# Two layers of a diffusion backbone on one core: modulation sums ordered behind the row scaling, the gate row multiplied ahead of the row factor, attention masks grouped, four weight differences on GpSimd

## The chip, the cores and the metric

The kernel runs on one core of a Trainium2 chip. The metric is the device time of one execution in microseconds (us); the time before is the median of three runs. The profile is one execution, taken by the hardware profiler.

## The reference, cut to what matters

512 tokens of width 1024 (256 context, 256 latent) go through two layers. Each layer is half-step SwiGLU, token mixer, half-step SwiGLU; every part is normed before and after, scaled and shifted by modulation vectors, and gated by one:

```python
def modulate(h, g_pre, shift, scale):
    return rms_norm(h, g_pre) * (1 + scale) + shift

def modulation(cond, w, b):                      # w: 1024 x 9*1024 per layer
    m = jax.nn.silu(cond) @ w + b

def half_ffn_update(h, mod, k, g_pre, g_post, w_in, w_out):
    y = swiglu(modulate(h, g_pre, mod[3 * k], mod[3 * k + 1]), w_in, w_out)
    return h + FFN_RES_WEIGHT * mod[3 * k + 2] * rms_norm(y, g_post)
...
x = x + mx[5] * rms_norm(yx, g[4])               # after the mixer
```

The mixer of layer 0 is a gated linear recurrence in both directions (RG-LRU), that of layer 1 is windowed attention (16 heads of 64, 4 key heads, a sink per head). The context has its own modulation. D_FF is 2816. All is float32. Only the latent half is returned.

## The kernel before, in words

**Precision.** Every large matmul is done as three: a value is split into a rounded high part (ScalarE copies it to fp32r, `split`, L113) and the rest (VectorE subtracts the high part). A weight slot (`wslot`, L117) is one load of 128 x 1024 floats into one of five `raw` buffers, a cast `whi` on ScalarE (L114) and a difference `wlo` on VectorE (L115), in one of eight slots. Activations are held as `hh` and `hl`.

**Tiling.** The tokens are four tiles of 128 rows: tiles 2 and 3 are latent (LAT), 0 and 1 context (CTX), worked in the order 2, 3, 0, 1. An FFN (L446) first does four blocks of 128 columns of the gate and up products for LAT, then the same four for CTX (a unit is 24 matmuls of 128x256), then the other 18 blocks for all tokens, in three groups; after each group the rows are multiplied by that part of `w_out` and added into `y`.

**Boundary.** In the last group, `out_last` (L427) finishes tile after tile; `after(t)` then calls `post` (L204: square and sum on ScalarE, an inverse root by small steps on VectorE (`rstd`, L175), product with the gate row and the row factor, add into the residual `x`) and `pre` (L218: square, inverse root, and the row scaling `scaled`, L192, whose last instruction is L194). The eight transposes of the scaled tile (`turn`, L197, matmul L201) follow as `pre_turn` some units later; ScalarE then applies scale and shift (L239) and the split makes `hh` and `hl`, which the next stage multiplies. So the next stage's LAT units start while the CTX tiles are still being normed.

**Modulation.** The next parts' modulation vectors are computed beside the FFN, as jobs (`mod_job`, L354) from which a step function takes one piece after each block or unit. A job clears two accumulators (one for each condition, memset L359; they lie in the two `m4` buffers), puts the bias into row 0 by a DMA from GpSimd's queue, and then for each of 8 rows of weight blocks loads 128 x 1024 floats and adds them times a per-partition scalar (L365, one for each condition). The column sums are matmuls with ones (L371). A gate row (`f` given) is multiplied by the norm's weights and written to DRAM, from where it is later read as a row for all partitions; a shift or scale is copied by ScalarE (L392) and transposed to columns (L280, then L396).

**Order.** The kernel is written against a framework that lays out each engine's queue when the kernel is built: a planner simulates the engines and takes the instruction that is ready and of highest priority; `pre` and `post` run at high priority. Semaphores are set by it. Each engine then runs its queue in order. Weight and modulation loads are all issued by SyncE, in its queue's order.

**Attention.** `soft` (L866) makes the scores of four heads and 128 queries in eight steps: for each of two pairs of heads two products of 64 rows (L877), two matmuls that add the mask through the identity (L879), then row maximum, exponential, and sum. Transposes and value products of the step before last stand between.

**Last FFN.** `last_ffn` (L957) starts with the token tiles as stationary operand and eight weight slots; at its end `finish` (L977) norms each tile, adds the residual and stores it.

The lines around which the change turns:

```python
for c in conds:
    v.scalar_tensor_tensor(acc[c], raw, self.cs[:, k, c : c + 1], acc[c], op0=ALU.mult, op1=ALU.add)
...
nc.vector.scalar_tensor_tensor(tmp, ysrc, r, grow[cond], op0=ALU.mult, op1=ALU.mult)
nc.vector.tensor_tensor(self.x[:, t], self.x[:, t], tmp, op=ALU.add)
```

Of the kernel before, what the change touches and what calls it, by code (L numbers as in the profile page):

```python
# [36 lines left out]
class Net:  # L37
    def __init__(self, ctx, tc):
# [4 lines left out]
        self.pending = []  # L43
        e = ctx.enter_context
# [68 lines left out]
    def split(self, hi, lo, src):  # L113
        self.nc.scalar.copy(hi, src)  # L114
        self.nc.vector.tensor_tensor(lo, src, hi.bitcast(F32), op=ALU.subtract)  # L115

    def wslot(self, srcs):  # L117
# [9 lines left out]
        self.split(hi[:, :n], lo[:, :n], raw[:, :n])  # L127
# [64 lines left out]
    def scaled(self, t, xs):  # L192
        r = self.rstd([self.mean_sq(xs, self.x[:, t])])
        self.nc.vector.tensor_scalar(xs, self.x[:, t], r, RS, op0=ALU.mult, op1=ALU.mult)  # L194
        return xs
# [157 lines left out]
    def mod_job(self, l, m, conds=(0, 1), f=None):  # L353
# [7 lines left out]
        for k in range(NK):  # L361
            raw = self.raw()
            nc.sync.dma_start(raw, self.w_mod[l, k * P : (k + 1) * P, m * D : (m + 1) * D])
            for c in conds:
                v.scalar_tensor_tensor(acc[c], raw, self.cs[:, k, c : c + 1], acc[c], op0=ALU.mult, op1=ALU.add)  # L365
            yield
        ps = self.st()
# [10 lines left out]
        if f is not None:  # L378
            gq = self.s2()
            gi = 3 + m // 3  # L380
            for j in range(4):
                cc = slice((j // 2) * 512, (j // 2) * 512 + 512)
                nc.gpsimd.dma_start(gq[32 * j : 32 * j + 32], self.norm_g[l, gi : gi + 1, cc].to_broadcast((32, 512)))
            row = self.a2()
# [713 lines left out]
```

## Time and profile before

| what | value |
|---|---|
| median of 3 runs | 1713.89 us (1711.07 to 1714.55) |
| the profiled execution | 1710.77 us, of which 1709.0 us span |
| TensorE busy | 1658.0 us (97%) |
| VectorE busy | 1118.7 us (65%) |
| ScalarE busy | 704.7 us (41%) |
| GpSimd busy | 44.2 us (3%) |
| loads | 253 MB, 148 GB/s on average |

The span is the time from the first to the last event that the profiler saw on the core. PE is TensorE (PEld its weight loads), DVE VectorE, ACT ScalarE, POOL GpSimd, SP SyncE; a q behind a name (SPq) means its sequencer. A line such as L115 is one of the kernel's source lines; a helper such as `split` has one line for all its callers, and the tile names tell them apart. `PEclk` is the clock granted to TensorE as a share of 2.4 GHz.

### The profile page before, as it was taken

The page shows a single profiled execution, that of the slowest core. Times are in us where ns is not written, and L with a number is a line of the kernel's source. Part 1 is how long each engine was busy: PE and PEld are TensorE (multiplying, and loading weights), DVE is VectorE, ACT ScalarE, POOL GpSimd, SP SyncE. Part 2 cuts the span into 40 slices and gives each one's busy share as a digit, 9 for nine tenths or more (in the row PEclk, how much of TensorE's full clock was granted, in tenths as well). Part 3 has the DMA queues.
Part 4 walks back from the last instruction along what each step waited for, and adds up shares of the span by engine and source line. Part 5 has one row for each costly group of instructions (what it writes and reads, how often), then busy time and mean ns, then how long its engine had stood idle before and what let it go on. Part 6 is the DMA issues. An engine that isn't in the chain of part 4 may idle for free.

```text
span 1709.0 us, 22391 instructions
## 1 busy us (share of the span) xinstructions
PE 1658.0 (97%) x8744; PEld 1385.9 (81%) x8744; DVE 1118.7 (65%) x1705; ACT 704.7 (41%) x1117; POOL 44.2 (3%) x89
## 2 busy tenths in 40 slices
PE   6999999999999989999999999999999999999997
PEld 4978888888988788888888888878888886679997
DVE  4878677658978785877833695655433687575454
ACT  3423322236699442332222442332232466574442
POOL 0010000000000001000000001000000000000000
PEclk9999999999999999999999999999999999999999
DMA  9366655443233154666433055865332061046561
GB/s 341 132 207 214 202 174 177 147 162 99 79 95 99 50 198 133 211 205 198 156 116 98 26 197 164 293 197 172 108 109 96 29 218 50 1 152 210 169 202 45
DMA packets 163961, 253.39 MB, mean 148 GB/s; under 512 B 9600, under 2 KB 114664, under 8 KB 163856
## 3 DMA queue, kind: packets, MB, share of 16 engines
q1 hardware_dynamic: 159424, 244.35, 43.8%
q0 software_dynamic: 3680, 7.10, 1.4%
q8 instruction: 68, 1.11, 0.3%
q10 hardware_dynamic: 752, 0.53, 0.1%
q14 instruction: 37, 0.30, 0.1%
HBM read 250.84 MB, written 1.10 MB: 147 GB/s over the span
## 4 chain that ended last, share of the span: by engine, by line
PE 77%; DVE 10%; ACT 5%; DMA 5%; issue 2%; ACTq 0%; DVEq 0%
PE mm L151 15%; PE mm L153 15%; PE mm L152 15%; PE mm L166 7%; PE mm L168 7%; PE mm L167 7%; DVE m L365 3%; DMA raw<-in_w_mod_dram 2%; DVE wlo L115 2%; PE mm L877 1%; DMA raw<-in_ffn_w_out_dram 1%; DMA raw<-in_ffn_w_in_dram 1%; ACT whi L114 1%; PE st L914 1%; PE st L903 1%
## 5 line engine op out<-in xcount | busy, mean ns | idle before, releaser
L151 PE MATMUL mm<-hh,whi 128*128 128x512 f32 (+1 forms) x1808 | 615.8, 342 | 8.3 <-ACT hh L271 4.7
L152 PE MATMUL mm<-hl,whi 128*128 128x512 f32 (+1 forms) x1808 | 615.7, 341 | 1.4 <-DVE hl L115 1.0
L153 PE MATMUL mm<-hh,wlo 128*128 128x512 f32 (+1 forms) x1808 | 616.3, 341 | 0.3 <-DVE wlo L115 0.3
L115 DVE TENSOR_TENSOR wlo<-raw,whi 128x1024 fp32r<-128x1024 f32 x316 | 382.4, 1221 | 157.0 <-ACT whi L114 155.3
L114 ACT CAST whi<-raw 128x1024 fp32r<-128x1024 f32 x316 | 330.2, 1053 | 353.4 <-DMA raw<-in_ffn_w_in_dram 107.5
L151 PEld LDWEIGHTS mm<-hh,whi 128*128 128x128 f32 x1808 | 346.0, 192 | 54.4 <-ACT hh L271 5.4
L152 PEld LDWEIGHTS mm<-hl,whi 128*128 128x128 f32 x1808 | 346.5, 192 | 39.5 <-DVE hl L115 1.4
L153 PEld LDWEIGHTS mm<-hh,wlo 128*128 128x128 f32 x1808 | 346.8, 192 | 38.1 <-DVE wlo L115 0.6
L365 DVE SCALAR_TENSOR_TENSOR m<-raw,cs,m 128x1024 f32<-128x1024 f32 x224 | 277.0, 1278 | 47.1 <-DMA raw<-in_w_mod_dram 39.2
L166 PE MATMUL mm<-whi,dh 128*128 128x512 f32 x592 | 232.7, 393 | 4.7 <-ACT dh L114 2.4
L168 PE MATMUL mm<-whi,dl 128*128 128x512 f32 x592 | 231.2, 391 | 0.0
L167 PE MATMUL mm<-wlo,dh 128*128 128x512 f32 x592 | 231.0, 390 | 0.0
L413 DVE TENSOR_TENSOR a<-s,mm 128x512 f32<-128x512 f32 (+1 forms) x96 | 54.5, 568 | 171.0 <-PE mm L153 111.8
L166 PEld LDWEIGHTS mm<-whi,dh 128*128 128x128 f32 x592 | 111.6, 188 | 34.0 <-issue 3.4
L412 ACT ACTIVATE s<-mm 128x512 f32<-128x512 f32 (+1 forms) x96 | 48.3, 503 | 214.1 <-PE mm L153 214.1
L168 PEld LDWEIGHTS mm<-whi,dl 128*128 128x128 f32 x592 | 111.6, 188 | 23.9 <-DVE dl L115 0.4
L167 PEld LDWEIGHTS mm<-wlo,dh 128*128 128x128 f32 x592 | 111.5, 188 | 22.4
L114 ACT CAST dh<-a 128x512 fp32r<-128x512 f32 (+1 forms) x96 | 50.5, 526 | 187.6 <-DVE a L413 187.6
L115 DVE TENSOR_TENSOR dl<-a,dh 128x512 fp32r<-128x512 f32 (+1 forms) x96 | 54.6, 569 | 26.5 <-ACT dh L114 26.3
L239 ACT ACTIVATE tmp<-st,modT,A 128x128 f32<-128x128 f32 x144 | 54.6, 468 | 9.3 <-PE st L201 9.3
L482 DVE TENSOR_TENSOR y<-y,mm 128x512 f32<-128x512 f32 x24 | 16.5, 686 | 38.1 <-PE mm L168 38.1
L172 ACT ACTIVATE tmp<-y 128x1024 f32<-128x1024 f32 x12 | 12.7, 1058 | 58.5 <-DVE y L434 58.5
(212 smaller groups left out, 1311.6 us busy)
## 6 DMA issues: line engine op xcount, KB each, us to landing
raw<-in_ffn_w_in_dram SPq DMA_DIRECT2D x176, 512.0 KB, 4.8
raw<-in_w_mod_dram SPq DMA_DIRECT2D x128, 512.0 KB, 4.4
raw<-in_ffn_w_out_dram SPq DMA_DIRECT2D x88, 512.0 KB, 4.8
wm<-in_w_mod_dram SPq DMA_DIRECT2D x16, 512.0 KB, 7.2
raw<-in_rg_w_in_dram SPq DMA_DIRECT2D x16, 512.0 KB, 3.3
raw<-in_attn_w_qkv_dram SPq DMA_DIRECT2D x12, 512.0 KB, 3.7
g<-spill POOLq DMA_DIRECT2D x16, 256.0 KB, 4.4
raw<-in_rg_gate_w_dram SPq DMA_DIRECT2D x16, 256.0 KB, 3.2
```

Of the source, the lines that this page charges most:

```text
L114: self.nc.scalar.copy(hi, src)
L115: self.nc.vector.tensor_tensor(lo, src, hi.bitcast(F32), op=ALU.subtract)
L151: nc.tensor.matmul(out, a, xh, start=first and k == ks[0], stop=False, skip_group_check=True)
L152: nc.tensor.matmul(out, a, xl, start=False, stop=False, skip_group_check=True)
L153: nc.tensor.matmul(out, b, xh, start=False, stop=last and k == ks[-1], skip_group_check=True)
L166: nc.tensor.matmul(out, a, wh, start=(k == 0), stop=False)
L167: nc.tensor.matmul(out, a, wl, start=False, stop=False)
L168: nc.tensor.matmul(out, b, wh, start=False, stop=(k == nk - 1))
L239: nc.scalar.activation(hf[:, k * P : (k + 1) * P], ps[:, q * P : (q + 1) * P], AF.Identity, bias=S[:, k, cond : cond + 1], scale=A[:, k, c ...
L365: v.scalar_tensor_tensor(acc[c], raw, self.cs[:, k, c : c + 1], acc[c], op0=ALU.mult, op1=ALU.add)
L412: nc.scalar.activation(a, pg, AF.Silu)
L413: nc.vector.tensor_tensor(b, a, pu, op=ALU.mult)
```

## The change

1. `mod_job`: the sums (L365) are traced in a block that tells the planner to queue them on VectorE behind `self.chain`, the row scaling of the tile that was normed last. In the first FFN there is none yet.
2. The column sum of a job (`mod_sum`) and the transposes to columns (`mod_cols`) are no longer pieces of the job. They are put into a list and done at the start of the next step each; a job so has 8 pieces instead of 9 or 10. Behind the last group the list is emptied.
3. `post` and `finish`: VectorE multiplies `y` by the gate row without waiting for the row factor; then one instruction multiplies by the factor and adds the residual. The squares' output goes to an `m4` buffer. `finish` stores the second half from ScalarE's queue.
4. A one-column Silu behind the last Gelu of the RG mixer and behind the last exponential of the attention.
5. `soft`: all four products of a step first, then all four masks.
6. Last FFN: of the first eight weight slots, the second and the fourth of each four have their difference on GpSimd.

```diff
     def post(self, t, ysrc, grow):
-        nc = self.nc
-        tmp = self.tmp()
-        cond = t // 2
+        v = self.nc.vector
+        g = grow[t // 2]
+        tmp, junk = self.tmp(), self.m4().rearrange("p a b -> p (a b)")
+        parts = []
         if isinstance(ysrc, list):
-            halves = [slice(cb * 512, cb * 512 + 512) for cb in range(2)]
-            r = self.rstd([self.mean_sq(tmp[:, cc], y) for cc, y in zip(halves, ysrc)])
-            for cc, y in zip(halves, ysrc):
-                nc.vector.scalar_tensor_tensor(tmp[:, cc], y, r, grow[cond][:, cc], op0=ALU.mult, op1=ALU.mult)
+            for cb, y in enumerate(ysrc):
+                cc = slice(cb * 512, cb * 512 + 512)
+                parts.append(self.mean_sq(junk[:, cc], y))
+                v.tensor_tensor(tmp[:, cc], y, g[:, cc], op=ALU.mult)
         else:
-            r = self.rstd([self.mean_sq(tmp, ysrc)])
-            nc.vector.scalar_tensor_tensor(tmp, ysrc, r, grow[cond], op0=ALU.mult, op1=ALU.mult)
-        nc.vector.tensor_tensor(self.x[:, t], self.x[:, t], tmp, op=ALU.add)
+            parts.append(self.mean_sq(junk, ysrc))
+            v.tensor_tensor(tmp, ysrc, g, op=ALU.mult)
+        r = self.rstd(parts)
+        v.scalar_tensor_tensor(self.x[:, t], tmp, r, self.x[:, t], op0=ALU.mult, op1=ALU.add)

     def pre(self, t, A, S, buf):
         with self.tc.high_priority():
             xs = self.scaled(t, buf)
+        self.chain = self.last
...
             for c in conds:
-                v.scalar_tensor_tensor(acc[c], raw, self.cs[:, k, c : c + 1], acc[c], op0=ALU.mult, op1=ALU.add)
+                with self.order(self.chain):
+                    v.scalar_tensor_tensor(acc[c], raw, self.cs[:, k, c : c + 1], acc[c], op0=ALU.mult, op1=ALU.add)
+            if k == NK - 1:
+                self.later.append(lambda: self.mod_sum(l, m, acc, f))
             yield
+
+    def mod_sum(self, l, m, acc, f):
...
+        if f is None:
+            row = self.s2()
+            nc.scalar.copy(row, ps)
+            self.later.append(lambda: self.mod_cols(l, m, row))
             return
...
+    def finish_later(self):
+        todo, self.later = self.later, []
+        for f in todo:
+            f()
...
         def step(n):
+            N.finish_later()
             while n > 0:
...
+    with N.order(prev):
+        sc.activation(N.small([P, 1]), c1[:, 0:1], AF.Silu)
...
-        for c in range(2):
-            ps = [N.mm() for _ in range(2)]
+        banks = [[N.mm() for _ in range(2)] for _ in range(2)]
+        for c, ps in enumerate(banks):
             for i in range(2):
                 half = slice(64 * i, 64 * i + 64)
                 nc.tensor.matmul(ps[i], qf[2 * g + c][half, qs], kk[g][half], start=True, stop=False)
+        for ps in banks:
             for i in range(2):
                 nc.tensor.matmul(ps[i][:, mc], identr, mask[:, qt], start=False, stop=True)
+        for c, ps in enumerate(banks):
...
+        if u == 7:
+            sc.activation(N.small([P, 1]), es[:, 0:1], AF.Silu)
...
-        for cb in range(2):
-            ss.append(N.mean_sq(tmp[:, cb * 512 : cb * 512 + 512], po[t, cb]))
-        r = N.rstd(ss)
+        tmp, junk = N.tmp(), N.m4().rearrange("p a b -> p (a b)")
         for cb in range(2):
             cc = slice(cb * 512, cb * 512 + 512)
-            v.scalar_tensor_tensor(tmp[:, cc], po[t, cb], r, grow[1][:, cc], op0=ALU.mult, op1=ALU.mult)
-            v.tensor_tensor(tmp[:, cc], tmp[:, cc], N.x[:, 2 + t, cc], op=ALU.add)
-            nc.sync.dma_start(out[0, t * P : (t + 1) * P, cc], tmp[:, cc])
+            ss.append(N.mean_sq(junk[:, cc], po[t, cb]))
+            v.tensor_tensor(tmp[:, cc], po[t, cb], grow[1][:, cc], op=ALU.mult)
+        r = N.rstd(ss)
+        for cb, q in ((0, nc.sync), (1, nc.scalar)):
+            cc = slice(cb * 512, cb * 512 + 512)
+            v.scalar_tensor_tensor(tmp[:, cc], tmp[:, cc], r, N.x[:, 2 + t, cc], op0=ALU.mult, op1=ALU.add)
+            q.dma_start(out[0, t * P : (t + 1) * P, cc], tmp[:, cc])
...
-    first = [N.wrows(vi, 0, NK, 0), N.wrows(vi, 0, NK, 0, DFF)]
+    first = [
+        [N.wslot([vi[:, k : k + 2, c0 : c0 + 512]], nc.gpsimd if k in (2, 6) else None) for k in range(0, NK, 2)]
+        for c0 in (0, DFF)
+    ]
```

## Rows read from the trace of the kernel before

**Rows 1.** The page's busy time of each engine (share of the span) xinstructions.
```profile
PE 1658.0 (97%) x8744; PEld 1385.9 (81%) x8744; DVE 1118.7 (65%) x1705; ACT 704.7 (41%) x1117; POOL 44.2 (3%) x89
```
**Rows 2.** Waits of TensorE: instruction <- releaser: us in total, times, longest.
```profile
PE st L201 <- DVE y L194: 5.7, 4, 2.5
...
PE st L280 <- ACT s L392: 2.6, 1, 2.6
...
PE st L201 <- DVE tmp L194: 1.9, 1, 1.9
PE st L201 <- DVE small L183: 1.6, 1, 1.6
PE mm L166 <- ACT hh L114: 1.6, 1, 1.6
```
**Rows 3.** Stretches: length, busy us (instructions) by engine, PEclk, DMA share, GB/s.
```profile
608.20:634.62 26.42, 20.10 (x165) 19.26 (x163) 26.42 (x47) 13.11 (x31) 0.00 (x0) 0.98 0.51 171
634.62:640.50 5.88, 5.88 (x28) 5.88 (x29) 3.03 (x3) 0.00 (x0) 0.00 (x0) 0.51 0.55 177
640.50:646.38 5.88, 5.88 (x52) 5.88 (x51) 1.90 (x3) 2.46 (x4) 0.00 (x0) 1.00 0.00 1
1009.40:1019.18 9.78, 5.64 (x25) 4.83 (x25) 9.78 (x14) 4.83 (x12) 0.00 (x0) 0.65 0.51 161
1143.19:1148.96 5.77, 3.18 (x10) 2.56 (x10) 4.44 (x7) 1.10 (x2) 0.00 (x0) 0.70 0.88 296
1148.96:1152.00 3.04, 3.04 (x15) 2.50 (x14) 0.00 (x0) 0.00 (x0) 0.49 (x1) 1.00 0.52 199
```
**Rows 4.** VectorE's sums by line in 608:637.7 (busy us, mean ns | idle before).
```profile
L365 DVE SCALAR_TENSOR_TENSOR m<-raw,cs,m 128x1024 f32<-128x1024 f32 x16 | 20.3, 1278 | 0.0
```
**Rows 5.** VectorE in order of time: start, us, instruction; RG mixer to FFN.
```profile
608.02 1.28 DVE L365 SCALAR_TENSOR_TENSOR m<-raw,cs,m 128x1024 f32<-128x1024 f32 x1
...
627.77 1.28 DVE L365 SCALAR_TENSOR_TENSOR m<-raw,cs,m 128x1024 f32<-128x1024 f32 x1
628.97 0.74 DVE L194 TENSOR_SCALAR y<-xres,small 128x1024 f32<-128x1024 f32 x1
```
**Rows 6.** SyncE's queue in order of time, the loads of block 4.
```profile
624.75 9.61 SPq L123 DMA_DIRECT2D raw<-in_ffn_w_in_dram  x4
```
**Rows 7.** TensorE in order of time, transposes in the two boundaries without sums.
```profile
433.02 1.09 PE L201 MATMUL st<-ident,y 128*128 128x128 f32 x8 [1.36 <-DVE y L194]
...
1374.50 1.09 PE L201 MATMUL st<-ident,y 128*128 128x128 f32 x8 [0.16 <-DVE y L194]
```
**Rows 8.** Line 359 alone: ns min/median/max, first and last start.
```profile
L359 DVE MEMSET m<- x28: 912/912/912, 65.2 to 1147.5; 128x1024 f32 x28
```
**Rows 9.** VectorE in order of time: a scan, then before the last FFN.
```profile
553.94 1.22 DVE L745 TENSOR_TENSOR_SCAN g<-m,s 128x512 f32<-128x512 f32 x1
...
1510.19 1.22 DVE L115 TENSOR_TENSOR wlo<-raw,whi 128x1024 fp32r<-128x1024 f32 x1
...
1512.33 1.22 DVE L115 TENSOR_TENSOR wlo<-raw,whi 128x1024 fp32r<-128x1024 f32 x1 [0.85 <-ACT whi L114]
...
1516.25 1.23 DVE L216 TENSOR_TENSOR xres<-xres,tmp 128x1024 f32<-128x1024 f32 x1
```
**Rows 10.** TensorE in order of time, products and masks of an attention step.
```profile
1448.71 1.12 PE L877 MATMUL mm<-dl,dh 64*128 64x512 f32 x2
1449.76 0.44 PE L879 MATMUL mm<-mask,identr 128*128 128x128 f32 x2
1450.13 1.13 PE L877 MATMUL mm<-dl,dh 64*128 64x512 f32 x4
```
**Rows 11.** VectorE in order of time, the end of the kernel.
```profile
1704.38 1.28 DVE L986 TENSOR_TENSOR tmp<-tmp,xres 128x512 f32<-128x512 f32 x2
```
**Rows 12.** The chain of waits in order of time, 585 to 650 us: start, us, what.
```profile
600.54 5.12 DMA raw<-in_ffn_w_in_dram
605.73 1.06 ACT whi L114
```

More of the change, by code (lines that the diff above doesn't have):

```diff
@@ L43, in __init__ @@
         self.pending = []
+        self.later = []
+        self.chain = None
         e = ctx.enter_context
@@ L111, in raw, with split, wslot @@
         return self.rawp.tile([P, D], F32, tag="raw", name=self.nm("raw"))
-    def split(self, hi, lo, src):
+    def split(self, hi, lo, src, eng=None):
         self.nc.scalar.copy(hi, src)
-        self.nc.vector.tensor_tensor(lo, src, hi.bitcast(F32), op=ALU.subtract)
-    def wslot(self, srcs):
+        (eng or self.nc.vector).tensor_tensor(lo, src, hi.bitcast(F32), op=ALU.subtract)
+    def wslot(self, srcs, eng=None):
         nc = self.nc
@@ L126, in wslot @@
         lo = self.wp.tile([P, D], F32R, tag="wlo", name=self.nm("wlo"))
-        self.split(hi[:, :n], lo[:, :n], raw[:, :n])
+        self.split(hi[:, :n], lo[:, :n], raw[:, :n], eng)
         return hi, lo
@@ L193, in scaled @@
         r = self.rstd([self.mean_sq(xs, self.x[:, t])])
-        self.nc.vector.tensor_scalar(xs, self.x[:, t], r, RS, op0=ALU.mult, op1=ALU.mult)
+        self.last = self.nc.vector.tensor_scalar(xs, self.x[:, t], r, RS, op0=ALU.mult, op1=ALU.mult)
         return xs
@@ L377, in mod_job, with mod_cols @@
                 )
[L378 to L384, printed above, removed]
-            v.scalar_tensor_tensor(row, ps, f * RS, gq, op0=ALU.mult, op1=ALU.mult)
-            spill = self.tc.dram_tile([4, 512], F32, name=self.nm("spill"))
-            nc.gpsimd.dma_start(spill, row[0:P:32])
-            self.rows[l, m] = spill
-            yield
-            return
-        row = self.s2()
-        nc.scalar.copy(row, ps)
-        yield
+        if f is None:
+            row = self.s2()
+            nc.scalar.copy(row, ps)
+            self.later.append(lambda: self.mod_cols(l, m, row))
+            return
+        gq = self.s2()
+        gi = 3 + m // 3
+        for j in range(4):
+            cc = slice((j // 2) * 512, (j // 2) * 512 + 512)
+            nc.gpsimd.dma_start(gq[32 * j : 32 * j + 32], self.norm_g[l, gi : gi + 1, cc].to_broadcast((32, 512)))
+        row = self.a2()
+        v.scalar_tensor_tensor(row, ps, f * RS, gq, op0=ALU.mult, op1=ALU.mult)
+        spill = self.tc.dram_tile([4, 512], F32, name=self.nm("spill"))
+        nc.gpsimd.dma_start(spill, row[0:P:32])
+        self.rows[l, m] = spill
+    def mod_cols(self, l, m, row):
         tv = self.cols_of(row)
         for hb in range(2):
-            v.tensor_copy(self.modT[:, l, m, hb * 4 : hb * 4 + 4, :], tv[:, :, 64 * hb : 64 * hb + 64 : 32])
-        yield
+            self.nc.vector.tensor_copy(
+                self.modT[:, l, m, hb * 4 : hb * 4 + 4, :], tv[:, :, 64 * hb : 64 * hb + 64 : 32]
+            )
+    def finish_later(self):
+        todo, self.later = self.later, []
+        for f in todo:
+            f()
     def pre_cols(self, l, k, conds=(0, 1)):
@@ L469, in ffn @@
                 bg(1000)
+                while self.later:
+                    self.finish_later()
                 rows()
```

3 lines of the change are left out of this document (2 added, 1 removed).

## The prediction

> **What bounds the kernel now.** I read the page's busy shares first, then who TensorE waited for, then short stretches around each of its waits, and last what the other engines did there. The reader is to see that TensorE is busy 97% of the span [rows 1], so no engine's total matters: what can be won is TensorE's idle time and the slow stretches behind it. Its longer waits, leaving out the kernel's start, lie mostly in places that the change touches: the transposes of a freshly normalised tile wait for the row scaling (L194), the matmuls after them for the ScalarE casts, one transpose for a modulation row [rows 2]. Four places carry nearly all of it.
>
> After the RG mixer, from 608.2 us, TensorE stands idle 26.42 - 20.10 = 6.3 us, and then runs 28 matmuls in 5.88 us at a granted clock of 0.51 where the next 5.88 us at 1.00 hold 52: 5.88 x (1 - 28/52) = 2.7 us more. Loss 9.0 us. Between the two FFNs at 1009 us, 25 instructions take 9.78 us at a mean clock of 0.65; at 5.88/52 = 0.113 us a matmul (17 of them) and about 1.1 us for the 8 transposes they need 3.0. Loss 6.8 us. At 1143 us 10 instructions take 5.77 us; at 3.04/15 = 0.20 us each they need 2.0. Loss 3.8 us [rows 3]. Before the last FFN it is 1.9 us for the scaled tile and 1.6 us for its cast [rows 2]. The slow stretches are at the lower of the two levels (0.51 of 2.4 GHz is 1.2 GHz), each behind some microseconds in which TensorE stood still; without the standstill I expect them to go as well.
>
> **Sums behind the row scaling.** In both boundaries the 16 sums of the next FFN's first job (20.3 us of VectorE in the first one) stand between the small steps of the last tile's chain [rows 4]. After the RG mixer 11 of the 16, the first at 608.02 and the last at 627.77, run before the scaling at 628.97 [rows 5]: 11 x 1.2 = 13 us of delay. Behind the chain they leave it free to end near 616 us, some 8 us before the lat half is through (8 units of 24 matmuls at 0.113 us from 602 on: 624 us). The sums then last until 616 + 20.3 + 3.4 (the GLU steps of four blocks) = 640 us. What that pushes: they hold the five raw buffers longer, and the SyncE queue has the four loads of block 4 behind the modulation rows, issued over 9.6 us [rows 6]. Those loads need the buffers of the sums before the last ones, so they land by about 640, casts and differences follow, and TensorE wants block 4 only after 16 units, near 646 with its transposes. So it is hidden, with a cover of some 4 us; if that is gone, each microsecond costs one, in either boundary. What is late next: two boundaries have no sums, and there the transposes stand in mid half and wait 1.36 and 0.16 us [rows 7]. I leave 2.0 us of the 9.0 (the 1.6 us for tile 0 come from weight loads and stay in part [rows 2]) and 1.2 of the 6.8. **-7.0 and -5.6 us**; bounds -9.0 and -6.8 (all gone) to -1.7 and -2.5 (only the waits for the scaling go: of the 5.7 us, less 1.36 and 0.16).
>
> **Sums and columns one step later.** Now the transposes of a modulation row may follow its column sum at once, and the copy between them stood behind other ScalarE work. A step is at least a unit of 24 matmuls at 0.20 us, 4.9 us, more than the 2.6 waited [rows 2, 3]. **-3.8 us**, bounds -3.8 and 0 (the wait turns up at another row). A job takes 8 steps, not 9 or 10, so loads come earlier but no step holds more. The accumulators share their buffers with the new scratch of the post step, so the memsets of the next FFN's first job (0.91 us, two in each of two boundaries [rows 8]), which could run ahead of the boundary, may fall into it: bounds 0 and 3.6 us, I take **+1.0**, as the chain leaves more room than that.
>
> **Gate row ahead of the row factor.** Per tile, VectorE's work stays (one product, one multiply-add), but the product lies beside ScalarE's square, and the separate add of 1.2 us [rows 9] leaves the chain. In the two big boundaries this is counted above. In the boundary before the RG mixer it bites on the 1.36 us [rows 7]: **-0.7**, bounds -1.4 and 0 (the planner moves the transposes up by as much). The attention constants lie in the buffers that post now uses as scratch, so their loads wait for a square: one load, with the q products of a whole tile as cover, nothing; uncovered it is one load of about 5 us.
>
> **Masks grouped.** Eight steps. In a late step the two heads of the first product pair are split by transposes: one alone (two records) takes 1.12 us, two together (four records) 1.13, so the split loses a whole 1.1; a mask pair takes 0.44 [rows 10]. Four masks with one weight should save one change of weights, about 0.2 us (half a mask pair) a step, 1.6 in all. Splits that vanish would add 4 x 1.1; a row maximum that comes 1 us later, and a copy and a transpose behind it, would cost up to 1.1 in five steps. I take some of the first: **-2.0**, bounds -6.0 and +4.
>
> **Last FFN.** Two weight differences, the second late for its cast by 0.85 us, stand before the small steps of the second tile, and the add of 1.2 is behind them [rows 9]. Without the one that goes to GpSimd (1.2), its wait and the add the scaling ends 3.2 us earlier, and TensorE waits 1.9 for it: **-1.9**. The 1.6 us for the cast stay, since the transposes still directly precede it. GpSimd's price is in no row. Its nearest are VectorE's same difference, 1.22 us, and a scan of half the elements in 1.22 [rows 9]: 1.2 to 2.5 us each. I take 2.5, and the four are still done before their matmuls. Bounds: -3.5 (the cast's wait too) and +3 (one difference late by its length). The Silu tables move to times when ScalarE idles: nothing, and 1.3 us where it doesn't.
>
> In the Trainium skill, GPSIMD Engine Reference (3.1 Elementwise - side-by-side cycle accounting) gives this operation 1.96 times VectorE's time, by an estimate from our row 2.4 us; no run here shows it, and the sum would be the same.
>
> **End.** After TensorE's last matmul come square, small steps, two products, two adds. The adds start at 1704.38 and last 1.28 [rows 11]; the products now lie beside the square and one pair is left. **-1.3**, bounds -2.0 and -0.7.
>
> **Sum.** -7.0 - 5.6 - 3.8 + 1.0 - 0.7 - 2.0 - 1.9 - 1.3 = -21.3 us. The profiled execution took 1710.8 (1709.0 of span and 1.8 around it), so 1689.5 by that; it lies 3.1 below the median of three, 1713.9. Against the median: **1692.6 us**.
>
> **Rivals.**
> Cast still in the way (0.12): the planner leaves the transposes at the end of the lat half, so the cast waits and the slow clock stay in both boundaries. Against it: without sums they stand in mid half [rows 7]. The first two terms shrink from 12.6 to 4.2: 1701.0.
> Attention worse (0.11): the exponentials end 1 us later, and the copies behind them hold the transposes. +4 for -2: 1698.6.
> GpSimd holds VectorE (0.10): the two take turns where both read SBUF, and each small step of the tile's chain has two inputs there. The chain then waits for one or two differences of 2.5 us: the 1.9 is not won, up to 3 lost: 1697.5. No row has GpSimd computing, so none speaks for or against.
> The Trainium skill states such turns in SBUF - State Buffer (Who interferes with whom): the shared port pair is an exclusive lock, and a VectorE instruction with two SBUF inputs contends with a GpSimd one that reads SBUF.
> Slower (0.06): one mechanism, TensorE's queue. Its order is fixed when the kernel is built; with shorter chains the planner puts the transposes earlier, while on the chip the small steps stand behind weight differences whose loads are late: a load of 5.12 us on the chain, a cast of 1.06 [rows 12] and a difference of 1.22 are 7.4 us in each of four boundaries, 29.6 less the 3.2 already left: 1719. From a mean of 6 us a boundary on it decides against the change; the 1.36 and 0.16 [rows 7] speak against it.
> The change doesn't do what it says (0.05): if the sums were put behind an older instruction they stay where they are, the small terms of either sign cancel: about 1712.
>
> **How the numbers follow.** Likeliest 0.56, its own range 1686 to 1700. All but the last two cases are faster by over 0.2% (3.4 us, about what a measurement of this kernel can tell from no change): 0.89; same 0.05; slower 0.06. The range takes in the first four cases with their bounds: 1684 to 1705.
>
> **What would show it.** Right: no sum (L365) between the small steps of the last tile's chain near 600 to 630 and 990 to 1012 us, the transposes in mid half, the clock at 1.00 there; no wait for the modulation row; the wait for the scaling before the last FFN gone, its cast wait left; one product pair at the end. Wrong: the idle of these places in other rows, above all long waits of the transposes in mid half, or of block 4 for its weights; GpSimd differences far above 2.5 us; attention steps longer than now.

## The result, and the profile after

The changed kernel takes 1702.2 us (median of 6 runs, 1700.3 to 1704.0) against 1711.5 beside it (6 runs): ratio 0.9945, interval 0.993 to 0.996, 9.3 us less. The forecast was 21.3 less, 1692.6 us; the measurement lies in its range, but more than half of the forecast gain is missing. The profiled execution has a span of 1699.2 us, 9.8 below the one of before, and those 9.8 us are what is shared out here.

The page's busy line of the changed kernel answers to [rows 1]:

```profile
PE 1652.8 (97%) x8744; PEld 1379.6 (81%) x8744; DVE 1118.7 (66%) x1701; ACT 703.7 (41%) x1119; POOL 56.5 (3%) x93
```

TensorE's waits in the changed kernel (instruction <- releaser: us in total, times, longest) answer to [rows 2]; a line of the kernel before is some two lower there (L201 is now L203, L194 is L196):

```profile
PE st L203 <- DVE y L196: 6.2, 6, 2.9
...
PE st L203 <- DVE tmp L196: 3.9, 1, 3.9
PE mm L170 <- DVE dl L117: 2.3, 1, 2.3
...
PE mm L155 <- DVE wlo L117: 1.9, 3, 0.8
...
PE mm L169 <- DVE wlo L117: 1.2, 1, 1.2
```

The wait for the modulation row (2.6) is gone, and so are most of those at the two FFN boundaries. Of the first row's 6.2 us only 1.2 lie at the second of them; 2.86 are a new wait before the attention and 1.63 one inside the RG output (at 577.8 us). And the wait before the last FFN has doubled (1.9 to 3.9), and four waits for low parts (wlo, dl) are new. What follows them costs time, too. Stretches of the changed kernel (length, busy us by engine, PEclk, DMA share, GB/s) answer to [rows 3]:

```profile
603.00:630.00 27.00, 26.91 (x225) 26.56 (x224) 26.25 (x47) 13.48 (x32) 1.00 (x2) 1.00 0.52 173
630.00:636.00 6.00, 6.00 (x52) 6.00 (x51) 6.00 (x6) 2.34 (x4) 0.00 (x0) 1.00 0.64 209
...
1056.00:1059.00 3.00, 2.10 (x6) 1.67 (x7) 2.22 (x4) 0.00 (x0) 0.00 (x0) 0.78 1.03 390
1059.00:1062.00 3.00, 3.00 (x10) 2.38 (x9) 2.04 (x2) 1.92 (x3) 0.00 (x0) 0.65 1.04 383
...
1509.00:1512.00 3.00, 0.40 (x2) 0.43 (x3) 2.72 (x10) 0.43 (x1) 0.00 (x0) 0.95 0.00 0
1512.00:1515.00 3.00, 2.35 (x11) 1.95 (x10) 0.05 (x1) 2.32 (x7) 0.00 (x0) 0.50 0.00 0
```

Behind the RG mixer TensorE is busy for 26.91 of 27 us where it was for 20.10 of 26.42, and the stretch behind it runs at 1.00 and no longer at 0.51. The slow clock is now found elsewhere: behind the new 2.27 us wait at 1056.9 us and behind the 3.9 us before the last FFN.

For the rest, the starts of TensorE's product groups cut every kernel into the same stretches. Their lengths in us, from each profiled execution (A: head of the second FFN, from its first input product to its first output product; B: the rest of that FFN; C and D: the same of the third FFN; E: the attention up to its first projection product; F: projection and head of the last FFN; the ratio is to the kernel before, by the fast runs). Each batch of runs has its own runs of the kernel before beside it, with medians of 1710.9 to 1713.0 us, so runs of different batches are compared by their ratios:

| kernel | A | B | C | D | E | F | ratio (interval) |
|---|---|---|---|---|---|---|---|
| before | 80.57 | 302.45 | 78.23 | 305.58 | 100.06 | 66.38 | |
| changed | 71.29 | 305.44 | 72.44 | 305.66 | 102.46 | 67.40 | 0.9945 (0.9930 to 0.9960) |
| changed again | 71.25 | 306.99 | 72.60 | 303.93 | 102.58 | 68.97 | 0.9957 (0.9943 to 0.9970) |
| e1 no GpSimd | 71.43 | 304.51 | 72.40 | 303.32 | 102.90 | 63.49 | 0.9909 (0.9893 to 0.9925) |
| e2 own scratch | 72.51 | 304.70 | 72.97 | 301.97 | 100.89 | 67.42 | 0.9912 (0.9898 to 0.9925) |
| e3 pauses | 71.21 | 302.89 | 72.20 | 301.44 | 103.20 | 69.65 | 0.9912 (0.9898 to 0.9926) |
| e4 sums free | 72.66 | 306.12 | 73.88 | 303.74 | 104.20 | 69.83 | 0.9953 (0.9938 to 0.9967) |
| e5 masks apart | 71.19 | 307.69 | 72.57 | 303.64 | 102.59 | 71.13 | 0.9953 (0.9941 to 0.9965) |
| e6 old post | 72.79 | 305.96 | 72.39 | 303.23 | 100.40 | 71.51 | 0.9946 (0.9930 to 0.9962) |
| e7 three mends | 72.45 | 302.44 | 72.60 | 301.44 | 99.66 | 63.49 | 0.9878 (0.9864 to 0.9893) |
| e8 sums in job | 71.19 | 302.44 | 72.33 | 301.42 | 102.73 | 68.96 | 0.9914 (0.9902 to 0.9926) |
| e9 two mends | 72.09 | 305.40 | 72.55 | 301.97 | 100.77 | 63.49 | 0.9898 (0.9884 to 0.9911) |
| e10 both undone | 81.22 | 302.66 | 78.26 | 301.47 | 100.40 | 70.83 | 1.0001 (0.9989 to 1.0013) |
| e12 mends, sums free | 71.51 | 302.44 | 77.54 | 301.41 | 100.27 | 63.51 | 0.9900 (0.9886 to 0.9914) |

Before to changed: A -9.3, B +3.0, C -5.8, D +0.1, E +2.4, F +1.0, the boundary before the RG mixer -1.4, the end -0.7, all else +0.9: together -9.8. The second execution of the changed kernel repeats A, C and E within 0.2 us; B, D and F move by up to 1.7.

E and F are cut finer by two more instructions, the first score product of the attention and the last product of its projection (us):

| kernel | E up to the first score product | from there to the last projection product | the rest of F |
|---|---|---|---|
| before | 42.42 | 107.63 | 16.38 |
| changed | 44.98 | 106.06 | 18.83 |
| changed again | 45.07 | 106.06 | 20.42 |
| e1 no GpSimd | 45.41 | 105.99 | 14.99 |
| e2 own scratch | 43.42 | 106.04 | 18.85 |
| e5 masks apart | 44.96 | 107.83 | 20.93 |
| e7 three mends | 42.17 | 106.04 | 14.94 |

Before to changed: +2.6, -1.6 and +2.4.

### The profile page after: what moved, and what is told of

It reads as the page before. It is cut to its first block, busy times and chain, and to the rows that moved or that the text cites. A ratio compares the mean times of both kernels' runs of the same rounds, so it can differ in the third digit from the quotient of the medians.

```text
span 1699.2 us, 22395 instructions
## 1 busy us (share of the span) xinstructions
PE 1652.8 (97%) x8744; PEld 1379.6 (81%) x8744; DVE 1118.7 (66%) x1701; ACT 703.7 (41%) x1119; POOL 56.5 (3%) x93
## 3 DMA queue, kind: packets, MB, share of 16 engines
q10 hardware_dynamic: 1040, 1.06, 0.2%
## 4 chain that ended last, share of the span: by engine, by line
PE 41%; DVE 8%; DMA 5%; issue 4%; ACT 3%; POOL 0%; DVEq 0%; ACTq 0%; SPq 0%
PE mm L153 7%; PE mm L155 7%; PE mm L154 7%; PE mm L168 4%; PE mm L170 4%; PE mm L169 4%; DVE m L371 3%; DVE wlo L117 2%; DMA raw<-in_ffn_w_in_dram 2%; DMA raw<-in_ffn_w_out_dram 2%; ACT whi L116 1%; PE st L942 1%; PE st L1001 1%; PE st L1002 1%; PE st L1003 1%
## 5 line engine op out<-in xcount | busy, mean ns | idle before, releaser
L503 DVE TENSOR_TENSOR y<-y,mm 128x512 f32<-128x512 f32 x24 | 16.5, 686 | 40.6 <-PE mm L170 40.2
L453 DVE TENSOR_TENSOR y<-y,mm 128x512 f32<-128x512 f32 x24 | 16.4, 685 | 37.4 <-PE mm L170 37.4
```

## The experiments

**e1: where F went.** VectorE in the changed kernel before the last FFN (start, us, instruction), and GpSimd beside it:

```profile
1495.81 6.76 DVE L117 TENSOR_TENSOR wlo<-raw,whi 128x1024 fp32r<-128x1024 f32 x2
1502.50 0.68 DVE L215 TENSOR_TENSOR tmp<-mm,xres 128x512 f32<-128x512 f32 x1
1503.10 1.75 DVE L181 SCALAR_TENSOR_TENSOR small<-small,small 128x1 f32<-128x1 f32 x1
```

```profile
1491.80 2.40 POOL L117 TENSOR_TENSOR wlo<-raw,whi 128x1024 fp32r<-128x1024 f32 x1 [113.94 <-ACT whi L116]
1494.79 10.04 POOL L117 TENSOR_TENSOR wlo<-raw,whi 128x1024 fp32r<-128x1024 f32 x3 [0.58 <-DVE hl L117]
```

A GpSimd difference takes 2.40 us where it starts ahead of VectorE's and 10.04/3 = 3.35 among them; VectorE's own take 6.76/2 = 3.38 there and no longer 1.22 [rows 9], and a step on one column takes 1.75. The edit:

```
- [N.wslot([...], nc.gpsimd if k in (2, 6) else None) for k in range(0, NK, 2)]
+ [N.wslot([...]) for k in range(0, NK, 2)]
```

> The changed kernel, but all eight weight differences of the last FFN on VectorE again. Theory (GpSimd and VectorE hold each other up: in the changed kernel three VectorE differences beside the GpSimd ones took 7.90 us, and TensorE's wait for the scaled rows of the last tile grew from 1.90 to 3.90 us): no VectorE difference of this stretch takes over 1.6 us, the wait for the scaled rows falls to 2 us or below, and the kernel ends 1.5 to 3 us sooner, near 1699.5 us. Rival (the GpSimd work was needed, the wait grew because the post chain itself is longer): the wait stays near 3.9 us or grows by the 4.8 us of differences that come back to VectorE, time 1702 to 1705 us.

Measured 1696.9 us. VectorE in the same place of e1:

```profile
1495.26 2.36 DVE L117 TENSOR_TENSOR wlo<-raw,whi 128x1024 fp32r<-128x1024 f32 x2
...
1498.13 0.15 DVE L181 SCALAR_TENSOR_TENSOR small<-small,small 128x1 f32<-128x1 f32 x1
```

With four differences more to do, VectorE is sooner through: the differences take 1.2 us each again, the step on a column 0.15. TensorE's wait falls from 3.90 to 0.50 us and F to 63.49, 3.9 us less than in the changed kernel and 2.9 less than before; 1.5 of the 2.9 lie ahead of the last projection product and are not won by this edit, so the wait itself is worth 1.4 against before. The theory holds, and the time fell by 5.4 us where 1.5 to 3 were foreseen: 3.9 are F's, because the clock comes with the wait, and D, which moves by 1.7 between two executions of the changed kernel, is 2.3 shorter. In the nine kernels with GpSimd differences the wait is 3.3 to 4.1 us and a stretch behind it runs at a granted clock of 0.50; F is 67.4 to 71.5 us, in large part by how long that stretch lasts. In the four without, the clock stays at 1.00 and F is 63.5 in each.

**e2: the scratch of the post step.** The change lets the squares be written to a buffer of the ring m4, where modulation accumulators and the attention's constants live. Here they go to a tile of their own:

```
+ self.junk = self.const.tile([P, D], mybir.dt.bfloat16, tag="junk", name="junk")
- tmp, junk = self.tmp(), self.m4().rearrange("p a b -> p (a b)")
+ tmp, junk = self.tmp(), self.junk
```

> The changed kernel, but the squares of the post steps and of the end are written to a tile of their own (128x1024 bf16) and no longer to a buffer of the ring m4. Theory (the attention mixer's constants and its scratch wait for the ring's buffers, and the post chain of the last tile stands behind that wait on VectorE): the mask constants are loaded before the attention boundary, VectorE's wait of 1.76 us and the slow mask cast of 1.23 us leave the chain, TensorE's wait at the attention boundary falls from 2.86 us to under 0.5 us, and the time falls by 2 to 3 us, to about 1699.5 us. Rival (the wait is the post chain itself, whatever the scratch): the wait stays above 2 us and the time within 1 us of the changed kernel.

Measured 1698.2 us. ScalarE's queue issues the loads of the constants; first the changed kernel, then e2:

```profile
1362.80 0.37 ACTq L818 DMA_DIRECT2D m<-in_k_dram  x1
```

```profile
1167.20 0.36 ACTq L819 DMA_DIRECT2D m<-in_k_dram  x1
```

They start 196 us earlier, and what VectorE waited for in the changed kernel, ahead of and among the row factor's steps of the last tile, is gone. VectorE of the changed kernel there:

```profile
1369.27 0.42 DVE L846 TENSOR_TENSOR dh<-mm,m 128x256 f32<-128x256 f32 x1 [1.76 <-DMA m<-in_k_dram]
...
1370.27 0.14 DVE L183 TENSOR_SCALAR small<-small 128x1 f32<-128x1 f32 x1
1371.65 0.29 DVE L823 CAST mask<-m 128x256 fp32r<-128x256 f32 x1 [1.23 <-DMA m<-in_k_dram]
1371.86 0.15 DVE L185 TENSOR_SCALAR small<-small 128x1 int32<-128x1 int32 x1
```

E falls by 1.6 us, TensorE's wait from 2.86 to 0.91 (with 1.23 for a copy in its place, so not under 0.5). Not foreseen: the 2.27 us wait in D went as well. The ring does delay the modulation accumulators at the boundary: the memsets of the third FFN's first job start at 987.38 and 991.28 us in the changed kernel and before 900 us in e2. How that reaches the wait at 1056.9 us is not shown; memsets and loads near it are no earlier in e2.

**e3: pauses.** The change took the steps without a load from behind a modulation job. VectorE of the changed kernel ahead of the new 2.27 us wait:

```profile
1045.51 6.56 DVE L371 SCALAR_TENSOR_TENSOR m<-raw,cs,m 128x1024 f32<-128x1024 f32 x5
1051.99 0.68 DVE L432 TENSOR_TENSOR a<-s,mm 128x512 f32<-128x512 f32 x1
1054.96 1.28 DVE L371 SCALAR_TENSOR_TENSOR m<-raw,cs,m 128x1024 f32<-128x1024 f32 x1 [2.29 <-DMA raw<-in_w_mod_dram]
1056.16 0.69 DVE L117 TENSOR_TENSOR dl<-a,dh 128x512 fp32r<-128x512 f32 x1
```

and TensorE, which wants that dl:

```profile
1056.90 0.50 PE L170 MATMUL mm<-whi,dl 128*128 128x512 f32 x1 [2.27 <-DVE dl L117]
```

VectorE works in order: the low part of the GLU block stands behind a sum that waits for its modulation row. The edit puts one step without a load behind a gate row's job and two behind the others; the sums keep their new place:

```
             yield
+        for _ in range(1 if f else 2):
+            yield
```

> The changed kernel, but each modulation job again has one or two steps without a load behind its eight loads (9 or 10 steps, as before), while its sums and columns are still run at the start of the next step. Theory (the new waits of 0.8 to 2.3 us inside the FFNs come from eight loads of 512 KB following without a pause on SyncE's queue, with five raw buffers, so that weight differences stand in VectorE's order behind sums that wait for their rows): the waits of TensorE for weight lows inside the FFNs (0.81, 0.79, 1.21 and 2.27 us) mostly vanish and the time falls by 2.5 to 6 us, to 1696 to 1699.5 us. Rival (they come from the sums being ordered behind the scaling): they stay, and the time is within 1 us of the changed kernel.

Measured 1698.7 us. No wait of TensorE for a weight low of 0.3 us or more is left after the first FFN's start, B is 302.89 and D 301.44. The theory holds. With e2 this makes two mends for D, but of the two only the pauses bring B back to the 302.4 of before.

**e4, e6, e10: what won A and C.** Three kernels undo the ordering of the sums behind the scaling, the new post step, and both:

```
-                with self.order(self.chain):
+                with self.order(None):
```

```
-    v.tensor_tensor(tmp, ysrc, g, op=ALU.mult)
-r = self.rstd(parts)
-v.scalar_tensor_tensor(self.x[:, t], tmp, r, self.x[:, t], op0=ALU.mult, op1=ALU.add)
+    r = self.rstd([self.mean_sq(tmp, ysrc)])
+    nc.vector.scalar_tensor_tensor(tmp, ysrc, r, grow[cond], op0=ALU.mult, op1=ALU.mult)
+nc.vector.tensor_tensor(self.x[:, t], self.x[:, t], tmp, op=ALU.add)
```

> The changed kernel, but the modulation sums are free again to run ahead of the row scaling. Theory (this item won the two FFN boundaries, 9.3 and 5.8 us): both boundaries lose most of it again, TensorE waits 4 us or more at each, and the time rises by 8 to 14 us, to 1710 to 1716 us. Rival (the boundaries were won by the shorter post chain, with the product ahead of the row factor and no add): the boundaries stay within 2 us of the changed kernel's, and the time rises by less than 4 us. If the ordering is also what made the waits inside the FFNs, those (0.79, 1.21, 2.27 us) vanish here and take up to 4 us off the rise.

> The changed kernel, but the step behind each output projection is the old one: the gate row behind the row factor, an add of its own, the squares into the temporary (so nothing of it takes a buffer of the ring m4); sums still ordered behind the scaling. Without the ordering the two FFN boundaries lost only 1.4 us each. Theory (the shorter chain of this step is what won them): TensorE waits at both boundaries come back, the stretch from the last input product of the RG output to the first output product of the second FFN grows from 71.3 us to 76 us or more, the one at the third FFN from 72.4 to 75 us or more, and the time rises by 3 to 8 us. Rival (each of the two items is enough alone): both stretches grow by less than 2 us; then the time falls by up to 4 us, since the waits of 0.79, 1.21 and 2.27 us inside the FFNs and the late constants of the attention go with the ring's buffers free, to about 1698 us.

> The changed kernel with the old post step and without the ordering of the sums behind the scaling. Each alone cost 1.4 to 1.5 us at the boundary before the second FFN, where both together had won 9.3. Theory (either is enough): with both undone the stretch there grows by 7 us or more from 71.3 us, the one before the third FFN by 4 us or more from 72.4 us, TensorE's waits of 1.6 to 2.5 us return in both, and the time is 1706 to 1712 us. Rival (what won was something third, such as the later column step or the gate row's product): the stretches stay below 74 us and the time at 1699 to 1703 us.

Measured 1704.9, 1700.5 and 1712.6 us (e4's profiled execution is 4.0 us above its median). Undone alone, neither costs more than 1.5 us: A is 72.66 and 72.79, C 73.88 and 72.39, so the theory of e4 and the theory of e6 both fall. Undone together they take back all of A and C, 81.22 and 78.26, so the theory of e10 holds, with a time 0.6 us above its range. Its ratio of 1.0001 does not say that the rest of the change is worth nothing: D keeps 4.1 us, and F loses 4.5. Stretches of e10 against [rows 3]:

```profile
609.90:636.30 26.40, 19.83 (x161) 19.19 (x161) 26.37 (x47) 11.77 (x29) 0.00 (x0) 0.98 0.49 163
636.30:642.20 5.90, 5.89 (x27) 5.89 (x28) 3.03 (x3) 0.00 (x0) 0.00 (x0) 0.50 0.55 178
```

Why either is enough shows on VectorE. The modulation sums ahead of the last tile's row scaling, and when that scaling starts behind the start of A and of C (us):

| kernel | A: sums ahead | scaling | C: sums ahead | scaling |
|---|---|---|---|---|
| before | 11 of 16 | 26.8 | 9 of 16 | 26.1 |
| changed | 0 | 14.0 | 0 | 18.3 |
| e4 sums free | 5 | 21.3 | 5 | 23.1 |
| e6 old post | 0 | 15.2 | 0 | 16.3 |
| e10 both undone | 11 | 27.3 | 9 | 26.3 |
| e12 mends, sums free | 7 | 20.3 | 8 | 24.5 |

Either item brings the scaling forward by enough, and more than enough wins nothing. But e4 is not the shorter post step alone: its squares still take a buffer of the ring that holds the accumulators, whose memsets at C stand at 991.70 and 995.60 us, among the small steps of the last tile, and not before 900 us as in e12. So the sums start late though they are free. VectorE of e4:

```profile
995.60 0.91 DVE L364 MEMSET m<- 128x1024 f32 x1 [0.16 <-issue]
```

The three also separate B: it is 306.12 with the ring alone (e4), 305.96 with the ordering alone (e6), 302.66 with neither (e10), all with the close loads. So close loads did no harm by themselves there; with one more thing that delays the sums, which must free the raw buffers, B was over 3 us longer. In e6 the ring is free and E is 100.40; that the waits inside the FFNs would go with it, as its rival had it, did not come (B, and a wait of 1.17 us for a weight's low part at 763 us).

**e5: masks.** The four mask products stand again behind their own pair of scores:

```
-        banks = [[N.mm() for _ in range(2)] for _ in range(2)]
-        for c, ps in enumerate(banks):
+        for c in range(2):
+            ps = [N.mm() for _ in range(2)]
```

> The changed kernel, but the four mask products of an attention step stand again behind the two score products of their own pair. The forecast gave the grouping 2.0 us; in the changed kernel the step became only 0.09 us shorter and four new waits of 0.18 us a step stand in it. Theory (the grouping is worth about nothing, because what it saves in switches it gives back in waits for score banks): each step within 0.15 us of the changed kernel's 7.73 us, time within 1 us of the changed kernel. Rival (the grouping won its 2 us and something else in the stage took them): steps of 7.95 us or more and a time 1.5 to 2.5 us longer.

Measured 1702.7 us; E is 102.59 against 102.46, a late step 7.82 us against 7.73. TensorE in one step of the changed kernel, then of e5:

```profile
1438.39 0.66 PE L931 MATMUL st<-ident,dl 128*128 128x128 f32 x4 [0.18 <-ACT s L933]
1438.98 1.12 PE L901 MATMUL mm<-dl,dh 64*128 64x512 f32 x2
1440.03 0.66 PE L904 MATMUL mm<-mask,identr 128*128 128x128 f32 x4
```

```profile
1436.78 1.12 PE L901 MATMUL mm<-dl,dh 64*128 64x512 f32 x2
1437.83 0.44 PE L903 MATMUL mm<-mask,identr 128*128 128x128 f32 x2
1438.20 1.13 PE L901 MATMUL mm<-dl,dh 64*128 64x512 f32 x4
1439.26 0.44 PE L903 MATMUL mm<-mask,identr 128*128 128x128 f32 x2
```

The four masks cost 0.66 and not 0.88, as forecast (0.2 a step). But the score products are still split by transposes (2 records in 1.12 us), and a transpose now waits 0.18 us for a copy. A step gains 0.1 us, as the theory has it. But E ends at the first projection product, and the last steps lie among the projection's products behind it. From the first score product to the last projection product it takes 107.63 us before, 106.06 in the changed kernel and 107.83 here, while the other kernels with grouped masks agree within 0.1 us (e6 and e10 apart, where a product there waits 1.2 and 1.3 us for a weight). So the theory that the grouping is worth nothing falls: it won 1.6 to 1.8 us, most of it behind E, as the rival has it (the rival's steps of 7.95 us did not come). Where behind E it lies was not looked into. The time does not show it, because the rest of F moves by about as much between executions.

**e8: the place of the sums.** Sums in steps of their own behind the eight loads, as before; the columns still run at the start of the next call:

```
-            if k == NK - 1:
-                self.later.append(lambda: self.mod_sum(l, m, acc, f))
             yield
+        self.mod_sum(l, m, acc, f)
+        yield
```

> The changed kernel, but the column sums of a modulation job stand again in steps of their own behind its eight loads, at their old place in the order; sums still ordered behind the scaling, new post step. The forecast gave 3.8 us at one place of the second half of FFN three to moving them one step later. Theory (the place of the sums is worth these 3.8 us, and the missing pause costs the waits inside the FFNs): the wait of 3.8 us comes back, the waits of 0.79, 1.21 and 2.27 us go, time within 2 us of the changed kernel. Rival (the wait went for another reason): it stays away and the time falls by 3 to 4 us, to about 1698.5 us, as it did with pauses alone.

Measured 1695.9 us; B is 302.44, D 301.42, and no transpose waits for a modulation row. The theory about the sums' place falls: of the second item of the change, what removed the wait of [rows 3] at 1143 us is the columns. The order of the sums and the post step did not, as e10 has no such wait either. Before, a call of two steps could issue sum and columns behind one another, with no unit between.

**e9, e7, e12: mends together.** e7 joins the edits of e1, e2 and e3; e9 leaves out the pauses; e12 leaves out the ordering.

> The changed kernel with three mends at once: no differences on GpSimd, the squares into a tile of their own, one or two steps without a load behind each modulation job. Theory (they act in different places: GpSimd before the last FFN, the ring in the attention boundary and with the pauses inside the FFNs): 3.9 us at the last boundary, 1.6 us at the attention and some 3 us inside the FFNs add up to 7 to 9 us, time 1693 to 1696 us. Rival (the ring and the pauses mend the same waits, and what is won is given back in the clock): 5 to 6 us, 1696.5 to 1698 us.

> The version with three mends, but without the pauses behind the modulation jobs: no differences on GpSimd, the squares into a tile of their own, loads as close as in the changed kernel. The buffers of the ring and the pauses each took the waits inside the FFNs away when tried alone. Theory (the ring is the cause, the close loads do harm only with it): time within 1.5 us of the three mends, 1689 to 1691.5 us, and no wait over 0.5 us for weight lows inside the second to fourth FFN. Rival (both act): 1692 to 1694 us.

> The version with three mends, without the ordering of the sums behind the scaling. Theory (either of ordering and shorter post step is enough, and the ordering only delays the sums elsewhere): time within 2 us of the three mends, 1688.5 to 1692 us. Rival (the ordering still earns its 1.4 us at each FFN boundary): 1692 to 1695 us.

Measured 1689.8, 1693.5 and 1693.5 us. e7 is the fastest here, ratio 0.9878, 21.1 us below the kernel before beside it and some 3 us better than its expectation: with the standstills the slow stretches go (from 70 us on its granted clock is 1.00 throughout). TensorE before the last FFN in e7:

```profile
1500.46 1.06 PE L204 MATMUL st<-ident,tmp 128*128 128x128 f32 x8 [0.46 <-DVE tmp L197]
...
1503.54 0.50 PE L169 MATMUL mm<-whi,hh 128*128 128x512 f32 x1 [1.58 <-ACT hh L117]
```

and in the changed kernel:

```profile
1511.60 1.89 PE L203 MATMUL st<-ident,tmp 128*128 128x128 f32 x8 [3.90 <-DVE tmp L196]
...
1515.09 0.50 PE L168 MATMUL mm<-whi,hh 128*128 128x512 f32 x1 [0.74 <-ACT hh L116]
```

The same eight transposes take 1.06 us behind the short wait and 1.89 behind the long one. In e9 the theory falls (the ring alone is not the cause: B stays at 305.40 with the ordering and the close loads), the rival's 1692 to 1694 is met. In e12 the time lies in the rival's range, but not for the rival's reason: A holds without the ordering, and C goes back to 77.54, with a wait of 2.02 us for a cast and a granted clock of 0.50 behind it. So the shorter post step alone is enough for A and not for C. The table above shows why e4 did better at C: here the squares have a tile of their own, the accumulators are free long before, and eight sums go ahead of the scaling instead of five, which starts 1.4 us later. VectorE of e12:

```profile
982.85 1.28 DVE L372 SCALAR_TENSOR_TENSOR m<-raw,cs,m 128x1024 f32<-128x1024 f32 x1
```

That the pauses, the other difference near C, have no part in it was not tried.

**e11: the changed kernel again.**

> The changed kernel itself once more, beside the others on the same chip. All theories: a ratio to the kernel before of 0.993 to 0.996, 1700 to 1704 us; what is of interest is whether the weight waits inside the FFNs and the lower clock behind the 3.9 us wait before the last FFN come in the same places.

Measured 1703.1 us. The four weight waits come again in the same places (0.87, 1.07, 1.04 and 2.15 us), a fifth of 0.60 us is new at 764 us, and the 3.93 us wait comes again with its slow clock. They belong to the kernel, not to one execution. The slow stretch behind the 2.27 us wait does not: behind the 2.15 here the clock stays at 1.00, and D is 1.7 us shorter.

## Why the forecast was too large

Term by term, forecast against measured:

| term | forecast | measured | from |
|---|---|---|---|
| boundary behind the RG mixer | -7.0 | -9.3 | A |
| boundary between the FFNs | -5.6 | -5.8 | C |
| columns one step later | -3.8 | -4.1 | D in e7, no wait |
| ring and closer loads | +1.0 | +7.2 | B +3.0; D +0.1 in spite of the -4.1 (second execution: +7.0) |
| gate row, before the RG mixer | -0.7 | -1.4 | the stretch up to the RG output |
| attention constants | 0 | +2.6 | E up to the first score product |
| masks | -2.0 | -1.6 | from there to the last projection product |
| last FFN | -1.9 | +2.4 | the rest of F |
| end | -1.3 | -0.7 | |
| the rest | 0 | +0.9 | |

Three terms make the miss: the ring and the closer loads (6.2 us worse than forecast), the last FFN (4.3) and the attention's constants (2.6); the boundaries gave back some 3.

**Right.** TensorE's standstills and the slow clock behind them, as units, were the price to look at, and the two boundaries and the column wait were won almost as forecast: -19.2 for -16.4. The mechanism was right too: no sum stands ahead of the last tile's scaling any more, which after the RG mixer ends at 616.2 us (the forecast was near 616), and e6 shows that the ordering alone is enough. What I did not see is that the new post step does nearly the same alone (e4; in e12 at A only). A went further than -7.0 since the 1.62 us for tile 0 [rows 2], which I left in part to the weight loads, went too. The masks came out near their price (-1.6 for -2.0), though not in the late steps, where I looked for it: a step gained 0.1 us.

**Wrong: "loads come earlier but no step holds more".** This is the largest miss, 6.2 us. It looked at a step of the schedule and not at SyncE's queue and the five raw buffers. SyncE's queue in the changed kernel:

```profile
1025.64 14.23 SPq L125 DMA_DIRECT2D raw<-in_ffn_w_out_dram  x3
1045.62 4.17 SPq L368 DMA_DIRECT2D raw<-in_w_mod_dram  x4
1050.78 5.86 SPq L125 DMA_DIRECT2D raw<-in_ffn_w_out_dram  x3
```

and in e7:

```profile
1021.33 9.69 SPq L126 DMA_DIRECT2D raw<-in_ffn_w_out_dram  x3
1031.96 13.35 SPq L369 DMA_DIRECT2D raw<-in_w_mod_dram  x4
1046.31 3.01 SPq L126 DMA_DIRECT2D raw<-in_ffn_w_out_dram  x3
```

The four modulation loads between the weight groups are issued in 4.17 us and not in 13.35, the weights around them start 4.3 and 4.5 us later than in e7 (0.8 of it from the way up to there), and a sum that waits for such a load holds the GLU's low part on VectorE. Late weights alone are not it: in e2 they start at 1025.90 and 1053.95 us, and no wait of 0.5 us follows. I asked what waits for the loads and not what VectorE has queued behind the sums. The +1.0 for the ring was meant for memsets at the boundary. They do stand there now, but A and C are no longer than in e2; the ring's price was paid in the FFNs (D, e2) and in E.

**Wrong: attention constants "nothing".** I priced one load behind a square under a tile's products. Its consumers, however, sit on VectorE in the middle of the tile's row factor, and 1.76 + 1.23 us of waiting went into that chain. Without the ring E is 99.7 to 100.9.

**Wrong: the last FFN.** I took 2.5 us a difference, which 2.40 confirms, and put what they do to VectorE at nothing in the likeliest case. That is the step that failed: among them VectorE's own differences take 3.38 us instead of 1.22, and TensorE's wait is 3.90 instead of none. The rival with chance 0.10, that GpSimd holds VectorE, happened in this term. Its bound of 3 us lost was short: the second execution of the changed kernel lost 4.0 in the rest of F, since the slow clock behind the wait lasted longer. That the scaling would come 3.2 us earlier is not shown: without GpSimd the wait falls by 1.4 us, with the difference back on VectorE.

**Half right: the end.** The product was to lie beside the square. That is so where y is in SBUF (square from 982.75 us, product from 981.99); in PSUM it waits for it. VectorE of the changed kernel at the end answers to [rows 11]:

```profile
1686.15 0.69 DVE L1011 TENSOR_TENSOR tmp<-st,xres 128x512 f32<-128x512 f32 x1 [1.32 <-ACT m L174]
...
1692.22 0.68 DVE L1011 TENSOR_TENSOR tmp<-mm,xres 128x512 f32<-128x512 f32 x1
1692.82 0.15 DVE L181 SCALAR_TENSOR_TENSOR small<-small,small 128x1 f32<-128x1 f32 x1
...
1694.54 1.41 DVE L1015 SCALAR_TENSOR_TENSOR tmp<-tmp,small,xres 128x512 f32<-128x512 f32 x2
```

The Trainium skill, PSUM — Partial Sum Buffer (PSUM bank collisions raise a hardware error), says that the compiler orders any two engines' accesses to one bank and quadrant, two reads as well; the first row agrees: its product starts at 1686.15 us, when the square of the same tile (from 1685.43) is done. Two products are gone from behind the last row factor (-1.3). But VectorE is busy with the tile before until 1691.7 us, so the two products of the last tile stand ahead of its small steps, which start 0.6 us later behind TensorE's last matmul than before: -0.7.

The rivals on the cast, on attention steps (+4) and on TensorE's queue did not happen: the cast's waits at both boundaries are gone, the steps are no longer, and the transposes stand in mid half.

## What to carry to other kernels

When an edit takes pauses out of a background job or gives a ring one more user, price it on the in-order engine that consumes the job: list what stands there behind an instruction whose load has moved. When two edits attack the same wait, price them together once, since the second may add nothing. Cut the stretches where the work ends, not where the next stage begins: the gain of the masks lay behind the cut. A wait of TensorE is to be priced with the slow stretch that may follow it: three mends that took away waits of 1 to 4 us gave some 12 us more than the change alone.

## What the runs showed of the hardware

GpSimd and VectorE took turns by whole instructions. In e10 a GpSimd difference, then VectorE's small steps around it:

```profile
1510.72 2.39 POOL L117 TENSOR_TENSOR wlo<-raw,whi 128x1024 fp32r<-128x1024 f32 x1 [0.16 <-PE mm L170]
```

```profile
1508.24 2.35 DVE L181 SCALAR_TENSOR_TENSOR small<-small,small 128x1 f32<-128x1 f32 x1
...
1510.81 2.32 DVE L188 SCALAR_TENSOR_TENSOR small<-small,small 128x1 f32<-128x1 f32 x1
```

A step on one column, 0.22 us elsewhere, lasts until the GpSimd difference ends (1510.72 + 2.39 = 1513.11; the step ends at 1513.13). The product with one operand in PSUM (L215) took 0.68 beside GpSimd in the changed kernel, as it does without. The Trainium skill, SBUF — State Buffer (Who interferes with whom), says that a VectorE instruction with two SBUF inputs contends with a GpSimd instruction that reads SBUF, and calls the shared port pair an exclusive lock; these rows agree. So the harm of a GpSimd difference is not its own length but that a 0.2 us step of a critical chain takes 2.3.

The same wait was followed by the slow clock in one trace and not in another. In the changed kernel it came behind the wait of 2.27 us in D in one execution, and not behind the 2.15 us in the same place in the next. And every kernel here, the one before too, has a wait of 2.22 to 2.27 us at the start of the RG output, near 560 us. In six of the fourteen traces the granted clock behind it falls to 0.50 for some microseconds, in the other eight it stays at 1.00. So part of what two executions differ by is this, and from the length of a wait alone these rows do not tell whether a slow stretch follows.
